# Moving two PSUM evictions to ScalarE and half of the rotary pass to GpSimd in a three-mixer decoder trunk

## The chip, the cores and the metric

The kernel runs on one core of a Trainium2 chip. The metric is device time in microseconds (us) of one execution, median over several executions. The engines in the text are TensorE (PE; its weight loads are listed apart as PEld), VectorE (DVE), ScalarE (ACT), GpSimd (POOL) and SyncE (SP), which issues all the transfers.

## The reference, cut to what matters

Two layers. Each projects the normalised stream h (1024 x 1024) to all queries, keys, values and gates, runs three groups of attention heads beside each other (A: differential attention, four heads with two softmaxes each; B: forgetting attention; C: stick-breaking attention), gates each output, applies one output projection and a layer norm. What the change touches is group A:

```python
r1 = x1 * cos - x2 * sin          # rotary, on the first 16 of 64 columns of q and k
r2 = x2 * cos + x1 * sin
...
w  = p1 - lam * p2                # two causal softmaxes of one head
oa = w @ v
oa = oa * rsqrt(mean(oa ** 2) + eps) * subln_g * (1 - lam_init)
ya = oa * silu(ag)
```

## The kernel before, in words

Everything is in blocks of 128 rows; SEQ is eight blocks. A projection (`proj_cols`, lines 150 to 161) makes one 128-column piece of q, k or a gate, transposed, in two halves of 512 positions; each half is 24 matmuls (weights and stream are split in a high and a low part) into one of two `acc` banks of PSUM, and is then evicted by `evac`. For group A `evac` of `proj_heads` (lines 233 to 247) applies the rotary embedding: DVE shuffles partitions out of the bank (`xy`, line 239), multiplies the bank by the cosine (`praw`, line 240), multiplies `xy` by the sine (line 241), and adds (line 242). Then `split_rows` (lines 177 to 185) splits `praw` in a rounded high part (ACT, line 181) and a rest (DVE, lines 183 and 185). There are four heads, q and k, two halves and two layers: 32 rotary passes. The `xy` tile has one buffer, which the gates share (tag `gate`), `praw` has two.

Attention of head m of group A (`attn_a`, lines 282 to 347) has five stages per block i: `soft` (two score products into `S` banks, DVE row maxima with the mask added, line 264; ACT exponentials, line 296; DVE combines the two softmaxes: reciprocal, `c`, and the mix into `e`, lines 299 to 301), `turn` (PE transposes `e` into `T` banks, line 275, evicted by ACT or DVE into `wT`), `mix` (i + 1 matmuls into a `T` bank `O_A`, evicted by DVE into `ou`, line 317), `close` (every fourth block: ACT squares, POOL power, DVE scaling of `ou`, line 334), `emit` (every fourth block: PE transposes four `ou` into a `T` bank `To_A`, which DVE evicts into `y` times a per-partition factor, line 344). All of `T`, `O_A` and `To_A` share two PSUM banks (tag `T`, line 60).

`advance` (line 633) emits the stages of five blocks at once, with the lags of line 43, between projections of the next head, which `FOLLOW` (line 556) lists:

```python
LAG = (0, 1, 2, 3, 5)
ORDER = {"A": (4, 3, 2, 0, 1), ...}
"C1": ("qA0", "kA0", "gC0"), "A0": ("qA1", "kA1", "vA2", "gC1"),
"A1": ("qA2", "kA2", "gA0"), "A2": ("qA3", "kA3", "vB0", "gA1"),
```

The framework then orders each engine's instructions by a plan of its own, made from the dependencies and its estimates of cost: each engine runs its queue strictly in that order, and the order is not the order of the code (instructions of `soft` stand between those of a rotary pass). POOL's other work is the low part of every weight tile (`wlo`, line 135, 128 x 512), the power of `close`, and parts of groups B and of the output stage.

Of the kernel before, what the change touches and what calls it, by code (L numbers as in the profile page):

```python
# [10 lines left out]
AF = mybir.ActivationFunctionType  # L11
ALU = mybir.AluOpType
# [3 lines left out]
P = 128  # L16
# [32 lines left out]
def tile_trunk(ctx, tc, x, ln_in_g, ln_in_b, w_in, b_forget, lambda_q1, lambda_k1, lambda_q2,  # L49
               lambda_k2, subln_g, w_out, ln_g, ln_b, c_ident, c_mask, c_tri, c_rope, out):  # L50
    nc = tc.nc
# [10 lines left out]
    def big(tag, name, shape=(P, S), dt=F32):  # L62
        return sb.tile(list(shape), dt, tag=tag, name=name, bufs=bufs[tag])

    def bank(tag, name, shape=(P, HALF)):
        return ps.tile(list(shape), F32, tag=tag, name=name, bufs=pbufs[tag])
# [3 lines left out]
    def mm(*args, **kw):  # L70
        recent[0] = nc.tensor.matmul(*args, **kw).ins  # L71
# [66 lines left out]
    def load_w(layer, col, n, key, tags=("whi", "wlo")):  # L138
        kn = 4 if n == P else 2
        res = []  # L140
        for k in range(0, NK, kn):
            raw = big("wraw", f"wr_{key}_{k}", (P, kn, n))
            src = w_in[layer, k * P:(k + kn) * P, col:col + n].rearrange("(k p) c -> p k c", p=P)
            nc.sync.dma_start(raw, src)
            hi, lo = split_w(raw, (P, kn, n), f"{key}_{k}", tags)
            res += [(hi[:, j, :], lo[:, j, :]) for j in range(kn)]
        return res


    def proj_cols(hts, w, evac, key):  # L150
        for half in range(2):
            hhi, hlo = hts[half]
            acc = bank("acc", f"acc_{key}_{half}")
            for k in range(NK):
                whi, wlo = w[k]
                mm(acc, lhsT=whi, rhs=hhi[:, k, :], start=k == 0, stop=False)
                mm(acc, lhsT=whi, rhs=hlo[:, k, :], start=False, stop=False)
                mm(acc, lhsT=wlo, rhs=hhi[:, k, :], start=False, stop=k == NK - 1)
                yield 0.65
            evac(half, acc)  # L160
            yield 0.0
# [15 lines left out]
    def split_rows(src, dst, cols, scale):  # L177
        for s in range(2):
            a, b = slice(64 * s, 64 * s + 64), slice(64 - 64 * s, 128 - 64 * s)
            hi = dst[s][a, cols]  # L180
            nc.scalar.activation(hi, src[a], AF.Copy, scale=scale)
            if scale == 1.0:
                nc.vector.tensor_tensor(dst[s][b, cols], src[a], f32(hi), ALU.subtract)
            else:
                nc.vector.scalar_tensor_tensor(dst[s][b, cols], src[a], scale, f32(hi), ALU.mult, ALU.subtract)
# [34 lines left out]
    def proj_heads(layer, hts, col, is_q, key, rope, done, tags):  # L220
        scale = QSCALE if is_q else 1.0
        res = [[None, None], [None, None]] if is_q else [None, None]
        def dest(half):
            if is_q:
                for s in range(2):
                    res[s][half] = big("Q1", f"Q1_{key}_{s}_{half}", (P, HALF), F32R)
                return [res[s][half] for s in range(2)], slice(0, HALF)
            if half == 0:
                for s in range(2):
                    res[s] = big("K", f"K_{key}_{s}", (P, S), F32R)  # L230
            return res, slice(half * HALF, (half + 1) * HALF)

        def evac(half, acc):
            src = acc
            if rope is not None:
                hs = slice(half * HALF, (half + 1) * HALF)
                src = big("praw", f"praw_{key}_{half}", (P, HALF))
                other = big("gate", f"xy_{key}_{half}", (P, HALF))
                nc.vector.stream_shuffle(other, acc, PARTNER)
                nc.vector.tensor_tensor(src, acc, rope[0][:, hs], ALU.mult)  # L240
                nc.vector.tensor_tensor(other, other, rope[1][:, hs], ALU.mult)
                nc.vector.tensor_tensor(src, src, other, ALU.add)
            d, cs = dest(half)
            split_rows(src, d, cs, scale)
            if half == 1:
                done(res)
        yield from proj_cols(hts, load_w(layer, col, P, key, tags=tags), evac, key)


    def scores(i, kst, q1, q2, key):  # L250
        half, rows = i // 4, slice((i % 4) * P, (i % 4 + 1) * P)
        res = []
        for a, b in row_pieces((i + 1) * P):
            sc = bank("S", f"S_{key}_{a}")
            mm(sc[:, :b - a], lhsT=q1[half][:, rows], rhs=kst[:, a:b], start=True, stop=False)
            mm(sc[:, :b - a], lhsT=q2[half][:, rows], rhs=kst[:, a:b], start=False, stop=True)
            res.append((a, b, sc[:, :b - a]))
        return res
# [23 lines left out]
    def attn_a(layer, head, kst, q1, q2, v, vcol, y, nlam, sg):  # L282
        key = f"A{layer}{head}"
        z1 = tiny.tile([P, NB], F32, tag="z1", name=f"z1_{key}", bufs=2)
        ws, wts, ous = {}, {}, {}

        def soft(i):
            n = (i + 1) * P
            es = []
            for s in range(2):  # L290
                k2 = f"{key}_{i}_{s}"
                sc = scores(i, kst[s], q1[s], q2[s], k2)
                e = big("e", f"e_{k2}")
                nm = neg_max(sc, mask[:, D + P - n:], e, k2)
                z = z1[:, i:i + 1] if s == 0 else tiny.tile([P, 1], F32, tag="z2", name=f"z2_{k2}")
                nc.scalar.activation(e[:, :n], e[:, :n], AF.Exp, bias=nm, scale=-1.0, accum_out=z)  # L296
                es.append(e)
            c = tiny.tile([P, 1], F32, tag="c", name=f"c_{key}_{i}")
            nc.vector.reciprocal(c, z)
            nc.vector.scalar_tensor_tensor(c, c, nlam, z1[:, i:i + 1], ALU.mult, ALU.mult)  # L300
            nc.vector.scalar_tensor_tensor(es[0][:, :n], es[1][:, :n], c, es[0][:, :n], ALU.mult, ALU.add)
            ws[i] = es[0]
            return 2 * SCORE_US[i]

        def turn(i):
            wts[i] = transposed(ws.pop(i), i, f"{key}_{i}")
            return 0.11 * (i + 1)

        def mix(i):
            wt = wts.pop(i)  # L310
            o = bank("T", f"O_{key}_{i}")
            for j in range(i + 1):
                mm(o[:, :P], lhsT=wt[:, j * P:(j + 1) * P], rhs=v[:, j, vcol:vcol + P],
                                 start=j == 0, stop=j == i)
            if i % 4 == 0:
                ous[i // 4] = big("ou", f"ou_{key}_{i}", (P, 4, P))
            nc.vector.tensor_copy(ous[i // 4][:, i % 4, :], o[:, :P])  # L317
            return 0.22 * (i + 1)

        def close(i):  # L320
            if i % 4 != 3:
                return 0.0
            ou, cs = ous[i // 4], slice(i - 3, i + 1)
            t = big("sq", f"sq_{key}_{i}", (P, HALF))
            ss = tiny.tile([P, 4], F32, tag="ss", name=f"ss_{key}_{i}", bufs=2)
            rs = tiny.tile([P, 4], F32, tag="rsa", name=f"rsa_{key}_{i}", bufs=2)
            for b in range(4):
                nc.scalar.activation(t[:, b * P:(b + 1) * P], ou[:, b, :], AF.Square, scale=P ** -0.5,  # L328
                                     accum_out=ss[:, b:b + 1])
            nc.vector.scalar_tensor_tensor(rs, z1[:, cs], EPS, z1[:, cs], ALU.mult, ALU.mult)  # L330
            nc.vector.tensor_tensor(rs, rs, ss, ALU.add)
            nc.gpsimd.tensor_tensor(rs, rs, mhalf, ALU.pow)
            for b in range(4):
                nc.vector.tensor_scalar(ou[:, b, :], ou[:, b, :], rs[:, b:b + 1], None, ALU.mult)
            return 0.0

        def emit(i):
            if i % 4 != 3:
                return 0.0
            ou = ous.pop(i // 4)  # L340
            t = bank("T", f"To_{key}_{i}")
            for b in range(4):
                nc.tensor.transpose(out=t[:, b * P:(b + 1) * P], in_=ou[:, b, :], identity=ident)
            nc.vector.tensor_scalar(y[:, (i - 3) * P:(i + 1) * P], t, sg, None, ALU.mult)
            return 0.44

        return [(i, soft, turn, mix, close, emit) for i in range(NB)]

    def attn_pair(layer, kind, pair, kst, q1, q2, v, y, negc=None):
# [223 lines left out]
    for layer in range(DEPTH):  # L573
# [51 lines left out]
        for n, tag in enumerate(("cos", "sin")):  # L625
            t = big(tag, f"{tag}_{layer}")
# [21 lines left out]
        for u, steps in FOLLOW.items():  # L648
# [5 lines left out]
            y = ys[u] if kind == "C" else big("y", f"y_{key}")  # L654
# [81 lines left out]
```

## Time and profile before

| what | us |
|---|---|
| median of 3 executions | 1378.75 (1377.78 to 1380.84) |
| the profiled execution, its own time | 1378.63 |
| its span (first to last instruction) | 1376.8 |
| busy: PE, DVE, ACT, POOL | 1329.1, 855.8, 575.7, 306.9 |
| mean granted TensorE clock | 0.998 of full |

The span is what the trace covers; 1.8 us of the execution's time lie around it. Busy times of the engines overlap. In this program PE is busy nearly throughout, so that a wait of PE adds to the time directly.

### The profile page before, as it was taken

Reading aid. Unit: us, or ns where it says so; the run is one execution under the profiler, and the core shown is the slowest. Engines: PE = TensorE matmul, PEld = TensorE weight load, DVE = VectorE, ACT = ScalarE, POOL = GpSimd, SP = SyncE. Lnnn points to the kernel's source line nnn. Section 1 sums busy time; section 2 is a strip of 40 time slices with the busy share of each in tenths; the row PEclk is TensorE's granted clock in tenths of the full one; section 3 lists DMA queues with packets and bytes.
Section 4 is the critical chain, followed back from the end, with each engine's and each line's share of the span. In section 5 each row is a group of like instructions: output and inputs, shape, how many; then the busy total and the mean of one; then the engine's idle time right before and its main releaser. Section 6 shows DMA issues by size and latency. Waiting matters only on the chain.

```text
span 1376.8 us, 21869 instructions
## 1 busy us (share of the span) xinstructions
PE 1329.1 (97%) x8250; PEld 1129.3 (82%) x8250; DVE 855.8 (62%) x1898; ACT 575.7 (42%) x1325; POOL 306.9 (22%) x309
## 2 busy tenths in 40 slices
PE   5999999999999999999999999999999999999997
PEld 4878878987898888777898897889887988877886
DVE  6644476569765775856542537675878567667554
ACT  2344454435343544641214444444444445456200
POOL 3410201121202222123422111112111222221332
PEclk9999999999999999999999999999999999999999
DMA  7550211032204131343435211112122132233342
GB/s 259 168 147 22 58 43 55 25 85 53 67 17 108 47 84 55 95 149 118 132 124 145 55 36 50 55 47 54 54 62 51 48 92 62 62 100 108 121 140 83
DMA packets 115569, 114.87 MB, mean 83 GB/s; under 512 B 8644, under 2 KB 93576, under 8 KB 115464
## 3 DMA queue, kind: packets, MB, share of 16 engines
q1 hardware_dynamic: 115464, 113.48, 27.9%
q8 instruction: 65, 1.06, 0.3%
q14 instruction: 40, 0.33, 0.1%
HBM read 74.62 MB, written 22.05 MB: 70 GB/s over the span
## 4 chain that ended last, share of the span: by engine, by line
PE 42%; DVE 5%; issue 4%; DMA 1%; ACT 1%; POOL 0%; SPq 0%; DVEq 0%; ACTq 0%; POOLq 0%
PE aco_o L71 12%; PE acc_qA L71 3%; PE acc_ggA L71 3%; PE S_A L71 2%; PE O_A L71 2%; PE acc_kA L71 2%; PE acc_ggB L71 2%; PE acr_vvA L71 2%; PE acc_kB L71 2%; PE acc_ggC L71 2%; PE O_B L71 1%; PE acc_qB L71 1%; PE S_B L71 1%; PE acr_vvB L71 1%; PE acc_kC L71 1%
## 5 line engine op out<-in xcount | busy, mean ns | idle before, releaser
L71 PE MATMUL aco_o<-wo,yhi_o 128*128 128x512 f32 (+1 forms) x462 | 142.0, 389 | 0.0
L296 ACT ACTIVATE e_A<-e_A,nm_A 128x256 f32<-128x256 f32 (+7 forms) x128 | 98.9, 773 | 32.4 <-DVE nm_A L264 31.6
L71 PEld LDWEIGHTS aco_o<-wo,yhi_o 128*128 128x128 f32 x462 | 85.5, 188 | 19.1
L372 DVE TENSOR_TENSOR_SCAN f_C<-f_C,mask 128x128 f32<-128x128 f32 (+7 forms) x64 | 85.5, 1376 | 24.7 <-ACT f_C L370 24.5
L71 PE MATMUL acr_vvA<-whi_vvA,hT 128*128 128x256 f32 x512 | 95.0, 283 | 0.0
L71 PE MATMUL aco_o<-wo,ylo_o 128*128 128x512 f32 (+1 forms) x231 | 89.7, 388 | 0.0
L71 PE MATMUL S_A<-K_kA,Q_qA 128*128 128x384 f32 (+3 forms) x384 | 86.1, 358 | 0.0
L71 PE MATMUL acc_qA<-hT,whi_qA 128*128 128x512 f32 x256 | 82.6, 401 | 0.0
L71 PE MATMUL acc_ggA<-hT,whi_ggA 128*128 128x512 f32 x256 | 82.2, 400 | 0.0
L71 PE MATMUL acc_kA<-hT,whi_kA 128*128 128x512 f32 x256 | 82.2, 401 | 0.0
L71 PEld LDWEIGHTS acr_vvA<-whi_vvA,hT 128*128 128x128 f32 x512 | 79.6, 188 | 0.2
L71 PEld LDWEIGHTS O_A<-v_vA,wT_A 128*128 128x128 f32 x576 | 73.2, 194 | 3.4
L71 PE MATMUL O_A<-v_vA,wT_A 128*128 128x128 f32 x576 | 75.7, 277 | 0.0
L328 ACT ACTIVATE sq_A<-ou_A 128x128 f32<-128x128 f32 x64 | 19.9, 311 | 126.0 <-DVE ou_A L317 126.0
L71 PE MATMUL acr_vvA<-wlo_vvA,hT 128*128 128x256 f32 x256 | 72.1, 282 | 0.0
L264 DVE CUSTOM_DVE_ANT_0 e_A<-S_A,mask 128x512 f32<-128x512 f32 (+3 forms) x128 | 68.5, 554 | 2.8 <-PE S_A L71 1.2
L509 POOL TENSOR_TENSOR ylo_o<-yr_o,yhi_o 128x256 fp32r<-128x256 f32 (+2 forms) x48 | 41.1, 883 | 118.0 <-ACT yhi_o L508 118.0
L71 PEld LDWEIGHTS S_A<-K_kA,Q_qA 128*128 128x128 f32 x384 | 63.1, 191 | 5.0 <-issue 0.7
L370 ACT ACTIVATE f_C<-S_C 128x384 f32<-128x384 f32 (+3 forms) x96 | 40.3, 494 | 57.5 <-PE S_C L71 57.3
L364 ACT ACTIVATE e_B<-e_B,nm_B 128x1024 f32<-128x1024 f32 (+7 forms) x64 | 49.5, 775 | 30.8 <-DVE nm_B L264 30.8
L360 POOL TENSOR_TENSOR negc<-negc,mask 128x128 f32<-128x128 f32 x64 | 34.2, 537 | 116.5 <-DVE nm_B L264 91.1
L526 DVE SCALAR_TENSOR_TENSOR r_o<-r_o,aco_o 128x512 f32<-128x512 f32 (+1 forms) x33 | 22.1, 671 | 58.0 <-PE aco_o L71 58.0
(213 smaller groups left out, 3433.8 us busy)
## 6 DMA issues: line engine op xcount, KB each, us to landing
Q_qA<-Q_qA SPq DMA_DIRECT2D x64, 128.0 KB, 2.4
wor<-in_w_out_dram SPq DMA_DIRECT2D x32, 256.0 KB, 2.6
r_o<-h_dram SPq DMA_DIRECT2D x16, 512.0 KB, 3.3
h_dram<-x SPq DMA_DIRECT2D x8, 512.0 KB, 4.3
wr_vvA<-in_w_in_dram SPq DMA_DIRECT2D x16, 256.0 KB, 2.7
Q_qC<-Q_qC SPq DMA_DIRECT2D x32, 128.0 KB, 2.4
wr_qA<-in_w_in_dram SPq DMA_DIRECT2D x16, 256.0 KB, 2.9
wr_kA<-in_w_in_dram SPq DMA_DIRECT2D x16, 256.0 KB, 2.9
```

Of the source, the lines that this page charges most:

```text
L71: recent[0] = nc.tensor.matmul(*args, **kw).ins
L264: nc.vector.tensor_tensor_reduce(e[:, a:b], sc, other[:, a:b], -1.0, lowest, ALU.add, ALU.min, nm)
L296: nc.scalar.activation(e[:, :n], e[:, :n], AF.Exp, bias=nm, scale=-1.0, accum_out=z)
L328: nc.scalar.activation(t[:, b * P:(b + 1) * P], ou[:, b, :], AF.Square, scale=P ** -0.5, accum_out=ss[:, b:b + 1])
L360: nc.gpsimd.tensor_tensor(diag, diag, mask[:, D:], ALU.add)
L364: nc.scalar.activation(w[:, :n], w[:, :n], AF.Exp, bias=nm, scale=-1.0, accum_out=z)
L370: nc.scalar.activation(w[:, a:b], p, AF.Sigmoid, scale=-1.0)
L372: nc.vector.tensor_tensor_scan(fr, fr, mask[:, :n], 0.0, ALU.mult, ALU.max)
L509: nc.gpsimd.tensor_tensor(ylo[:, e0:e0 + en, :], raw, f32(yhi[:, e0:e0 + en, :]), ALU.subtract)
L526: nc.vector.scalar_tensor_tensor(r[:, c0:c1], r[:, c0:c1], ALPHA, acc, ALU.mult, ALU.add)
```

## The change

`O_A` and `To_A` are evicted by ACT and not by DVE; the product with the sine and the sum of the rotary pass are made by POOL and not by DVE. The operands, the shapes and the rest of the program stay.

```diff
@@ proj_heads, evac
                 nc.vector.stream_shuffle(other, acc, PARTNER)
                 nc.vector.tensor_tensor(src, acc, rope[0][:, hs], ALU.mult)
-                nc.vector.tensor_tensor(other, other, rope[1][:, hs], ALU.mult)
-                nc.vector.tensor_tensor(src, src, other, ALU.add)
+                nc.gpsimd.tensor_tensor(other, other, rope[1][:, hs], ALU.mult)
+                nc.gpsimd.tensor_tensor(src, src, other, ALU.add)
@@ attn_a, mix
-            nc.vector.tensor_copy(ous[i // 4][:, i % 4, :], o[:, :P])
+            nc.scalar.copy(ous[i // 4][:, i % 4, :], o[:, :P])
@@ attn_a, emit
-            nc.vector.tensor_scalar(y[:, (i - 3) * P:(i + 1) * P], t, sg, None, ALU.mult)
+            nc.scalar.activation(y[:, (i - 3) * P:(i + 1) * P], t, AF.Copy, scale=sg)
```

## Rows read from the trace of the kernel before

**Rows 1.** The page, part 1: busy us, share of the span, instructions.

```profile
PE 1329.1 (97%) x8250; PEld 1129.3 (82%) x8250; DVE 855.8 (62%) x1898; ACT 575.7 (42%) x1325; POOL 306.9 (22%) x309
```

**Rows 2.** Stages by windows: length, then busy (instructions) of PE, PEld, DVE, ACT, POOL.

```profile
962.00:1001.00 39.00, 36.67 (x210) 31.59 (x209) 31.34 (x85) 17.80 (x50) 7.32 (x6) 1.00 0.22 62
1001.00:1052.00 51.00, 49.38 (x265) 41.61 (x265) 40.40 (x101) 22.75 (x55) 8.91 (x7) 1.00 0.21 56
```

**Rows 3.** Waits of PE and its weight loads: us in total, times, longest.

```profile
PE T_A L275 <- DVE e_A L301: 5.1, 4, 1.9
PE T_A L275 <- DVE ou_A L317: 3.7, 6, 1.0
PE T_A L275 <- DVE y_A L344: 3.0, 2, 1.5
...
PEld T_A L275 <- DVE ou_A L317: 5.5, 6, 1.4
...
PEld T_A L275 <- DVE y_A L344: 3.4, 2, 1.7
```

**Rows 4.** Timeline, 1003 to 1009 us: start, length, instruction, idle before it.

```profile
1003.62 1.28 PE L71 MATMUL O_A<-v_vA,wT_A 128*128 128x128 f32 x10
...
1006.09 1.39 DVE L183 TENSOR_TENSOR K_kA<-praw_kA,K_kA 64x512 fp32r<-64x512 f32 x2
...
1008.42 0.44 PE L275 MATMUL T_A<-ident,e_A 128*128 128x128 f32 x2 [0.99 <-DVE ou_A L317]
```

**Rows 5.** Timeline, 1057 to 1063 us.

```profile
1058.22 0.60 PE L343 MATMUL To_A<-ident,ou_A 128*128 128x128 f32 x4
...
1059.26 1.29 ACT L181 ACTIVATE K_kA<-praw_kA 64x512 fp32r<-64x512 f32 x2 [3.01 <-DVE praw_kA L242]
...
1061.35 0.75 DVE L344 TENSOR_SCALAR y_A<-To_A,sg 128x512 f32<-128x512 f32 x1
...
1062.16 0.66 PE L275 MATMUL T_A<-ident,e_A 128*128 128x128 f32 x4 [1.51 <-DVE y_A L344]
```

**Rows 6.** Groups of instructions that the change moves: busy us, mean ns, idle before.

```profile
L317 DVE COPY ou_A<-O_A 128x128 f32<-128x128 f32 x64 | 18.3, 286 | 59.5 <-PE O_A L71 59.2
...
L241 DVE TENSOR_TENSOR xy_kA<-xy_kA,sin 128x512 f32<-128x512 f32 x16 | 12.5, 780 | 0.0
...
L344 DVE TENSOR_SCALAR y_A<-To_A,sg 128x512 f32<-128x512 f32 x16 | 11.9, 743 | 2.1 <-PE To_A L343 2.1
...
L242 DVE TENSOR_TENSOR praw_kA<-praw_kA,xy_kA 128x512 f32<-128x512 f32 x16 | 10.9, 684 | 0.1
```

**Rows 7.** Groups by form: ACT copies out of PSUM of the same shapes.

```profile
L277 ACT COPY wT_A<-T_A 128x512 f32<-128x512 f32 x40 | 22.8, 570 | 3.7 <-PE T_A L275 3.6
...
L277 ACT COPY wT_A<-T_A 128x128 f32<-128x128 f32 x8 | 2.1, 265 | 3.4 <-PE T_A L275 3.4
```

**Rows 8.** Timeline, 970 to 985 us, inside one rotary pass.

```profile
982.26 1.27 POOL L135 TENSOR_TENSOR wlo_qA<-wr_qA,whi_qA 128x512 fp32r<-128x512 f32 x1 [4.44 <-ACT whi_qA L134]
982.37 1.18 DVE L300 SCALAR_TENSOR_TENSOR c_A<-c_A,nlam,z_A 128x1 f32<-128x1 f32 x1
...
983.47 0.68 DVE L241 TENSOR_TENSOR xy_qA<-xy_qA,sin 128x512 f32<-128x512 f32 x1
984.07 0.60 DVE L301 SCALAR_TENSOR_TENSOR e_A<-e_A,c_A,e_A 128x384 f32<-128x384 f32 x1
...
984.74 0.44 PE L275 MATMUL T_A<-ident,e_A 128*128 128x128 f32 x2 [1.95 <-DVE e_A L301]
```

**Rows 9.** Line 300 by itself: ns minimum/median/maximum, first and last start.

```profile
L300 DVE SCALAR_TENSOR_TENSOR c_A<-c_A,nlam,z_A x64: 206/219/1231, 213.8 to 1160.3; 128x1 f32<-128x1 f32 x64
```

**Rows 10.** Line 239, the first of each rotary pass: ns, first and last start.

```profile
L239 DVE STREAM_SHUFFLE xy_qA<-acc_qA x16: 729/738/749, 160.9 to 1040.3; 128x512 f32<-128x512 f32 x16
...
L239 DVE STREAM_SHUFFLE xy_kA<-acc_kA x16: 723/740/747, 179.8 to 1054.9; 128x512 f32<-128x512 f32 x16
```

**Rows 11.** Waits of the weight loads in group C.

```profile
PEld T_C L275 <- DVE f_C L372: 0.2, 1, 0.2
```

## The prediction, made before the changed kernel was run

> **What bounds the kernel.** I read the busy shares first: PE is busy for 97% of the span, no other engine for more than 62% [rows 1]. So the time is PE's work, which the change leaves alone, plus PE's waits, and only a wait that goes or comes counts. Next, the stages: while heads 1 and 2 of group A run beside the projections of heads 2 and 3, DVE is busy for 31.3 of 39 us and 40.4 of 51 us, against ACT's 17.8 and 22.8 and POOL's 7.3 and 8.9 [rows 2]. That is where DVE can be late for PE, and the waits say so: the transposes `T_A` wait for DVE's mix `e_A` (5.1 us, four times), for its eviction `ou_A` (3.7 us, six times) and for its eviction `y_A` (3.0 us, twice) [rows 3]. Both layers show the same pattern, so half of each belongs to a layer.
>
> The last two are waits for a PSUM bank, not for data, and the timeline shows why they arise. `O_A` is finished at 1004.9, yet its bank is still taken at 1008.4, since DVE's queue has the split `K_kA` (1.39 us, two of them) and more ahead of the copy; PE stands still for 0.99 us [rows 4]. `To_A` is finished at 1058.8, its eviction starts at 1061.35, and PE waits 1.51 us [rows 5]. The waits for `e_A` are different: they end with the chain row maximum, exponential, `c`, mix [rows 8].
>
> **The change, part by part.**
>
> *What leaves DVE.* 64 copies of 0.286 us, 16 evictions of 0.743 us, and 32 passes of a product and a sum; at 0.780 and 0.684 us (the k half's means, a little above the q half's) those are 46.8 us [rows 6, 10]. In all 18.3 + 11.9 + 46.8 = 77 us of DVE's 855.8. None of it is a saving by itself; it pays only where DVE is late for PE.
>
> *What ACT gets.* The same shapes out of PSUM took ACT 0.265 and 0.570 us [rows 7]: 64 x 0.265 + 16 x 0.570 = 26 us, ACT then being at 602 us, or 44%. What hides it is ACT's idleness: in the example it sat idle for 3.01 us before 1059.26, waiting for the rotary sum [rows 5], and `To_A` was ready at 1058.8. Put there, the eviction would be over at 1059.4, long before PE asks at 1060.65 (1062.16 less 1.51). The reader of `ou`, the square of `close`, is on ACT already and loses a wait for another engine. DVE's 59.2 us of idling ahead of line 317 [rows 6] move to ACT; what is queued behind that wait there are exponentials of scores that PE makes after `O_A` anyhow, and casts of weights.
>
> The gain is thus the eight bank waits. PE's own idle rows give 3.7 + 3.0 = 6.7 us; the weight loads of the same transposes give 5.5 + 3.4 = 8.9 us [rows 3]. A busy PE row runs on to a modelled end, so the first is too small, and the second counts the load's own lead; I take the middle, **7.8 us**, and keep 1 to 8.9 as the ends. The low end is an ACT queue in which the eviction stands behind the two splits, so that the bank comes free about as late as now. What is late next, after the bank? In neither example the data: the first four transposes of the same weights had gone ahead in rows 4, and in rows 5 only the bank is named.
>
> *What POOL gets.* 32 products and 32 sums of 128 x 512. POOL's product-like instruction of that shape, `wlo`, took 1.27 us [rows 8], so 2.54 us a pass and 81 us in all, POOL going to 388 us of 1376.8. A pass, from shuffle to sum, becomes at least 0.74 + 2.54 = 3.3 us where DVE's four instructions need 0.74 + 3 x 0.6 to 0.7, about 2.7. The split and the swap transfers of q start 0.6 us later; they hide behind the value or gate projection that stands before the next head's first scores. The accumulator bank is freed by shuffle and cosine product, both still DVE's: nothing changes there. POOL's queue now has the passes between its `wlo`s; those wait for ACT's casts with 4.44 us to spare in the example [rows 8].
>
> *The port.* Here is what can spoil it. `c_A`, 128 x 1, takes 0.219 us as a rule, and 1.231 us at worst [rows 9]; in rows 8 it takes 1.18 us, starts while POOL's `wlo` runs (982.26 to 983.53) and ends with it. So a DVE instruction with both inputs in SBUF stands still until POOL's is through. [...]
>
> What it costs: DVE's order inside a pass is shuffle, cosine product, `c`, sine product, mix, sum. The cosine product reads PSUM and isn't held. After the change `c` comes to the port 0.6 us after POOL's product began and waits 1.27 - 0.60 = 0.67 us; the sine product's 0.60 us (983.47 to 984.07, [rows 8]) that stood ahead of the mix is gone. If DVE gets the port between POOL's product and its sum, the mix starts 0.07 us later than now: nothing. I take that, since no `c` was held for longer than one POOL instruction (1.231 - 0.219 = 1.0 us, [rows 9]). So the 5.1 us for `e_A` stay. The ends: they all go (-5.1), or the mix is held for the sum as well (below).
>
> In group C, 8 passes run beside scans that have two SBUF inputs, too. A scan held once is 1.0 us later; but PE waited for a scan a single time, 0.2 us [rows 11]. Ends 0 and 8; I take **1 us** for new waits there and elsewhere, nearer to the row with the slack.
>
> *Sum*, against the profiled execution's own 1378.63, which is 0.12 below the median: 1378.63 - 7.8 + 1.0 = **1371.8 us**.
>
> **The rivals.**
>
> 1. *Slower: the port is not given back between POOL's two instructions.* The sum is queued behind the product and its other input is long there, so it may take the port at once; then the mix waits for the sum also, 0.07 + 1.27 = 1.34 us later. `c` and the mix stand inside 10 of the 32 passes where DVE is behind (five a layer, the first at 973.2, the last at 1054.9 in the second). There PE waits for the mix already or nearly: 10 x 1.34 = 13.4 us, and 1378.63 + 13.4 - 7.8 + 1.0 = 1385.2. It decides from 6 such passes on. For it: the waits for `e_A`, up to 1.9 us [rows 3], lie in these very passes. Against: rows 9. [...]
> 2. *No change: the evictions are late on ACT as well.* ACT's splits wait for the rotary sum, which now comes from POOL, behind a `wlo` at times. If the plan puts the eviction after them, the bank is free at about 1061, as now. Gain 1, cost 1: 1378.6. For it: DVE's plan had it just so [rows 5]. Against: ACT's 3 us idle there.
> 3. *More: DVE's backlog dissolves.* With 77 us less, the `e_A` waits go also: 1378.63 - 8.9 - 5.1 = 1364.6. Against: these waits come from passes in which the port, not DVE's load, decides.
>
> That the change doesn't do what it says (an extra table load on ACT, say) is hardly open: copies with a scale and without run on ACT in this stage already.
>
> **How the numbers follow.** A difference of 0.2%, 2.8 us, is about what a measurement of this kernel can tell from none. Chances: forecast 0.45, rival 3 0.13, rival 2 0.22, rival 1 0.20. The forecast's own range is 1369.7 (8.9 gained, nothing new) to 1376 (6.7 gained, 4 us new). The range for 8 in 10 goes from rival 3's 1364 to 1384, just short of rival 1's full price. Faster: 0.45 + 0.13 = 0.58; within 0.2%: 0.22; slower: 0.20.
>
> **What would show it right or wrong.** Right: no wait of `T_A` for `ou_A` or `y_A`, on DVE or on ACT, worth 1 us; waits for `e_A` near 5 us; `c_A`'s median above 0.219 us, with holds of 0.7 us; rotary instructions of 1.27 us on POOL. Rival 1 shows as waits of `T_A` for `e_A` well over 10 us and a mix that starts after POOL's sum; rival 2 as waits of `T_A` for ACT's `ou_A` and `y_A`; rival 3 as no wait for `e_A`. It would be wrong altogether if PE's waits moved to weights (`wlo` late on POOL) or to the score products' queries.

## The result, and the profile after

The changed kernel takes **1394.3 us** (median of four runs, 1391.4 to 1397.0) against 1379.8 us for the kernel before (four runs). The ratio is 1.011, 95% interval 1.0087 to 1.0134: it is slower, by 14.5 us, where 1371.8 had been forecast. The profiled execution took 1391.38 us, with a span of 1389.6.

The page's busy shares after, the same lines as in [rows 1] and in the same columns:

```profile
PE 1338.2 (96%) x8250; PEld 1135.5 (82%) x8250; DVE 799.2 (58%) x1754; ACT 602.1 (43%) x1405; POOL 392.1 (28%) x373
```

DVE lost 57 us of busy time, ACT gained 26, POOL 85: the work moved as meant (77 us had been counted off DVE; the mixing and the scans took some back, below). PE's count is the same, but its rows are 9 us longer in all, and it stands still for longer. Its waits after the change (us in all, times, longest), which answer to [rows 3]:

```profile
PE T_C L275 <- DVE y_C L390: 6.9, 6, 1.5
PE O_A L71 <- ACT wT_A L277: 3.8, 4, 1.6
...
PE acr_vvB L71 <- ACT whi_vvB L134: 2.5, 2, 1.3
PE T_A L275 <- DVE e_A L301: 2.3, 2, 1.1
...
PE acr_vvB L71 <- POOL wlo_vvB L135: 2.0, 2, 1.0
```

The waits of `T_A` for `ou_A` are gone, and that for `y_A` is down to 0.3 us, as forecast. New ones took their place, and they are elsewhere: `T_C` in group C waits for the bank that DVE's `y_C` has to free, the products `O_A` wait for ACT's copies `wT_A`, and the value projection of group B waits for weights. The stage of group C in the first layer shows it, by windows (length, then busy time and instructions of PE, PEld, DVE, ACT, POOL; the figure behind POOL's is the granted clock, as a share of full speed). In the kernel before:

```profile
155.00:205.00 50.00, 49.58 (x326) 39.39 (x325) 37.04 (x50) 24.02 (x53) 5.52 (x4) 1.00 0.13 35
```

and in the changed kernel:

```profile
155.00:205.00 50.00, 45.91 (x292) 35.93 (x292) 30.03 (x40) 21.15 (x47) 15.31 (x12) 1.00 0.12 32
```

In the same 50 us PE gets 34 instructions less done, and is idle for 4.1 us instead of 0.4. And yet no engine is fuller than before, except POOL, which is at 15.3 of 50. So it is not a lack of engine time. DVE and ACT are both less busy, and both late. The timeline of one pass in that window shows one of the waits (start, length, instruction, and in brackets the idle time before it with what ended it):

```profile
161.31 1.28 POOL L241 TENSOR_TENSOR xy_qA<-xy_qA,sin 128x512 f32<-128x512 f32 x1 [9.40 <-DVE xy_qA L239]
...
162.67 1.28 POOL L242 TENSOR_TENSOR praw_qA<-praw_qA,xy_qA 128x512 f32<-128x512 f32 x1
...
163.37 0.44 PE L71 MATMUL O_C<-wT_C,dv 128*64 128x128 f32 x4
...
163.98 1.28 ACT L181 ACTIVATE Q_qA<-praw_qA 64x512 fp32r<-64x512 f32 x2 [4.11 <-POOL praw_qA L242]
...
164.64 1.41 DVE L185 SCALAR_TENSOR_TENSOR Q_qA<-praw_qA,Q_qA 64x512 fp32r<-64x512 f32 x2 [2.85 <-ACT Q_qA L181]
...
166.08 0.29 DVE L390 TENSOR_TENSOR y_C<-y_C,O_C 128x128 f32<-128x128 f32 x1
...
166.42 0.44 PE L275 MATMUL T_C<-ident,f_C 128*128 128x128 f32 x2 [1.50 <-DVE y_C L390]
```

POOL's two instructions end at 163.95. ACT's half of the split is next in ACT's queue and has waited 4.11 us for them; DVE's difference is next in DVE's queue and has waited 2.85 us for ACT's half. Behind it stands `y_C`, whose `O_C` was made at 163.8, and behind that PE. Neither queue passes over the instruction that waits.

But the delay alone isn't the whole of this wait. The same pass in the kernel before:

```profile
164.19 2.02 DVE L185 SCALAR_TENSOR_TENSOR Q_qA<-praw_qA,Q_qA 64x512 fp32r<-64x512 f32 x2 [0.70 <-ACT Q_qA L181]
...
165.06 0.71 PE L71 MATMUL acc_qA<-hT,whi_qA 128*128 128x512 f32 x2
...
166.07 0.40 PE L275 MATMUL T_C<-ident,f_C 128*128 128x128 f32 x2
...
166.24 0.29 DVE L390 TENSOR_TENSOR y_C<-y_C,O_C 128x128 f32<-128x128 f32 x1
```

`y_C` came 5.37 us after the shuffle of the pass then and comes 5.59 us after it now, 0.2 us later. What differs is PE's order. Before, four matmuls of the projection stood ahead of these `T_C`, which started before `y_C` and so did not wait for it; now they come first and do. In the last pass of the window it is DVE's order that differs. Before, `y_C` stood ahead of the split:

```profile
190.23 1.31 PE L71 MATMUL O_C<-wT_C,dv 128*64 128x128 f32 x20
...
191.62 0.29 DVE L390 TENSOR_TENSOR y_C<-y_C,O_C 128x128 f32<-128x128 f32 x1 [0.29 <-PE O_C L71]
...
192.02 1.41 DVE L183 TENSOR_TENSOR K_kA<-praw_kA,K_kA 64x512 fp32r<-64x512 f32 x2
```

and in the changed kernel it stands behind it, 3.2 us after its `O_C` was made instead of 0.1:

```profile
193.35 1.31 PE L71 MATMUL O_C<-wT_C,dv 128*64 128x128 f32 x20
...
196.42 1.40 DVE L183 TENSOR_TENSOR K_kA<-praw_kA,K_kA 64x512 fp32r<-64x512 f32 x2 [3.45 <-ACT K_kA L181]
...
197.86 0.29 DVE L390 TENSOR_TENSOR y_C<-y_C,O_C 128x128 f32<-128x128 f32 x1
...
198.20 0.44 PE L275 MATMUL T_C<-ident,f_C 128*128 128x128 f32 x2 [1.27 <-DVE y_C L390]
```

Of the six waits of `T_C` for `y_C`, the four longest (1.50, 1.49, 1.27 and 1.28 us over the two layers) are at these two places; the two of 0.7 us come with both orders as they were, and there `y_C` is 0.6 us later in its pass. So the plan that the framework makes anew for each kernel has a part in the loss: it puts work behind a split that then waits. No run keeps the old order with POOL in the pass, so how much is the longer pass and how much the new order stays open.

Over the 32 passes, the waits of the split's two sides (engine and line, what is waited for, us in all, times, longest), first on ACT:

```profile
ACT Q_qA L181 <- POOL praw_qA L242: 77.0, 16, 7.5
ACT K_kA L181 <- POOL praw_kA L242: 54.8, 16, 4.8
```

and on DVE:

```profile
DVE Q_qA L185 <- ACT Q_qA L181: 34.7, 12, 3.7
DVE K_kA L183 <- ACT K_kA L181: 25.9, 14, 3.5
```

ACT's 131.8 us were 53.4 before (then a wait for DVE's sum), DVE's 60.6 were 13.2. The groups of the kernel before (busy us, mean ns, idle before):

```profile
L183 DVE TENSOR_TENSOR K_kA<-praw_kA,K_kA 64x512 fp32r<-64x512 f32 x32 | 25.5, 798 | 6.3 <-ACT K_kA L181 5.4
...
L185 DVE SCALAR_TENSOR_TENSOR Q_qA<-praw_qA,Q_qA 64x512 fp32r<-64x512 f32 x32 | 24.5, 766 | 8.5 <-ACT Q_qA L181 7.8
...
L181 ACT ACTIVATE K_kA<-praw_kA 64x512 fp32r<-64x512 f32 x32 | 20.1, 629 | 25.1 <-DVE praw_kA L242 24.6
L181 ACT ACTIVATE Q_qA<-praw_qA 64x512 fp32r<-64x512 f32 x32 | 20.1, 629 | 29.1 <-DVE praw_qA L242 28.8
```

DVE gave away 46 us of products and sums, and 47 us of waiting at the head of its queue came in their place.

In the experiments, **theory 1** is this: the splits, in their order behind a pass that has become longer, hold the queues of DVE and ACT. **Rival 1** is what the prediction calls the port, though no run shows one: POOL's instructions make DVE's longer. **Rival 2** is its second as well: the evictions are late on ACT. Each time stands against the kernel before as run on the same chip.

### The profile page after: what moved, and what is told of

The parts are those of the page before. It is cut to its first block, busy times and chain, and to the rows that moved or that the text cites. A ratio compares the mean times of both kernels' runs of the same rounds, so it can differ in the third digit from the quotient of the medians.

```text
span 1389.6 us, 21886 instructions
## 1 busy us (share of the span) xinstructions
PE 1338.2 (96%) x8250; PEld 1135.5 (82%) x8250; DVE 799.2 (58%) x1754; ACT 602.1 (43%) x1405; POOL 392.1 (28%) x373
## 3 DMA queue, kind: packets, MB, share of 16 engines
q1 hardware_dynamic: 115464, 113.48, 27.6%
## 5 line engine op out<-in xcount | busy, mean ns | idle before, releaser
L372 DVE TENSOR_TENSOR_SCAN f_C<-f_C,mask 128x128 f32<-128x128 f32 (+7 forms) x64 | 87.9, 1413 | 24.9 <-ACT f_C L370 24.8
L301 DVE SCALAR_TENSOR_TENSOR e_A<-e_A,c_A,e_A 128x128 f32<-128x128 f32 (+3 forms) x64 | 62.6, 978 | 2.0
L71 PE MATMUL acr_vvB<-whi_vvB,hT 128*128 128x260 f32 x256 | 52.3, 299 | 3.9 <-ACT whi_vvB L134 2.5
```

The costliest lines, as they stand in the source:

```text
L372: nc.vector.tensor_tensor_scan(fr, fr, mask[:, :n], 0.0, ALU.mult, ALU.max)
```

## The experiments

**One half each.** The evictions alone (line 317, line 344):

```diff
-            nc.vector.tensor_copy(ous[i // 4][:, i % 4, :], o[:, :P])
+            nc.scalar.copy(ous[i // 4][:, i % 4, :], o[:, :P])
...
-            nc.vector.tensor_scalar(y[:, (i - 3) * P:(i + 1) * P], t, sg, None, ALU.mult)
+            nc.scalar.activation(y[:, (i - 3) * P:(i + 1) * P], t, AF.Copy, scale=sg)
```

> Both evictions (O_A and the transposed outputs) by ScalarE, the rotary pass left whole on VectorE. Theory 1 (the loss comes from the rotary pass alone: the two splits behind it wait in order for GpSimd's product and sum, and what is queued behind them on VectorE and ScalarE is late for TensorE): faster than before by 4 to 10 us, about 1372 us, with no wait of TensorE on ou_A and none of T_C on y_C over 1 us. Rival 2 (the evictions are late at the head of ScalarE's queue, also without the rotary change): not faster than before, 1379 us or more, with TensorE's waits on ou_A and y_A still there, now named ACT.

Measured: 1371.06 us against 1378.86, ratio 0.9932 (0.9909 to 0.9955): 7.8 us faster. No wait on `ou_A` is left, none of `T_C` for `y_C` is among PE's waits, and of `y_A` 1.3 us remain, now on ACT (PE's waits):

```profile
PE T_A L275 <- DVE e_A L301: 3.6, 2, 1.8
...
PE T_A L275 <- ACT y_A L344: 1.3, 2, 0.6
```

The rotary part alone (lines 241 and 242, `nc.vector` to `nc.gpsimd`):

> Sine product and sum of the rotary pass by GpSimd, both evictions left on VectorE. Theory 1: slower than before by 12 to 22 us, about 1396 us, with the waits of VectorE's splits on ScalarE's half at about 60 us in all (13 before) and T_C waiting for y_C by several us. Rival 1 (the port is held, every VectorE instruction beside GpSimd's gets longer): slower too, but by VectorE's own durations: the scans, the differences and the mixing of e_A beside a pass are each longer by 0.5 us or more. Rival 2: within 3 us of before.

Measured: 1403.31 us against 1378.86, ratio 1.017 (1.0138 to 1.0202): 24.5 us slower, beyond the upper end of what theory 1 gave. DVE's splits wait 61.5 us (37.1 + 24.4), and `T_C` waits 6.9 us for `y_C`. The two halves add up to +16.7, and the whole change cost +14.5. So rival 2 is out, and all of the loss is in the rotary part. On rival 1 this run is mixed: the mixing of `e_A` takes 62.6 us instead of 54.3 (0.13 us more each), the scans 87.9 instead of 85.5; both are longer, neither by the 0.5 us that rival 1 asked for.

**The splits moved out of the way.** The changed kernel, with the splits of a pass (and the swap transfers) issued behind DVE's and ACT's last instruction of the score step that comes next:

```diff
+            def rest(): split_rows(src, d, cs, scale); return done(res) if half == 1 else None
+            if rope is None: rest()
+            else: late.append(rest)
-            split_rows(src, d, cs, scale)
-            if half == 1:
-                done(res)
...
+            with tc.issue_after(tail['dve']) if behind else ExitStack():
+                with tc.issue_after(tail['act']) if behind else ExitStack():
+                    late.pop(0)()
```

> The changed kernel, whole, with one thing moved: the two splits of a rotary pass (and the swap transfers of q that follow them) are issued behind VectorE's and ScalarE's last instruction of the score step that comes next, so that they no longer stand ahead of work that is ready. GpSimd does as much at much the same times. Theory 1: most of the loss comes back, 1371 to 1382 us, the splits' waits fall from 132 us (ScalarE) and 61 us (VectorE) to under half, and T_C waits for y_C by under 2 us. Rival 1 (the port): as slow as the changed kernel, 1390 to 1397 us, for the port is held as long. Rival 2 (evictions late on ScalarE): no gain either.

Measured: 1370.25 us against 1378.86, ratio 0.9929 (0.9903 to 0.9954), just under the range. All of the loss is back, with POOL doing as much as in the changed kernel. ACT's wait for POOL's sum in the q passes is 3.4 us in all, for 77.0, and DVE's splits wait 2.0 us, for 60.6. ACT's wait:

```profile
ACT Q_qA L181 <- POOL praw_qA L242: 3.4, 6, 1.1
```

That speaks for theory 1, but not yet against rival 1: the place may be a gain of its own.

**POOL's load without the wait.** The kernel before, with two more instructions on POOL behind each sum, into a tile that nobody reads:

```diff
+                nc.gpsimd.tensor_tensor(idle, src, rope[1][:, hs], ALU.mult); nc.gpsimd.tensor_tensor(idle, idle, src, ALU.add)
```

> The kernel before, whole, with two more 128x512 instructions of GpSimd (a product and a sum) behind each rotary pass, into a tile that nobody reads: GpSimd's load of the change without the wait on it. Theory 1: within 3 us of before, 1377 to 1382 us, with the splits' waits as before (13 us on VectorE). Rival 1 (the port): slower by 8 us or more, near the changed kernel.

Measured: 1430.0 us against 1378.86, ratio 1.0363 (1.033 to 1.0396), 51 us slower. Theory 1 was wrong here, and by far. The splits' waits are as before (7.8 and 6.4 us), but the splits themselves have become longer (busy us, mean ns, idle before):

```profile
L183 DVE TENSOR_TENSOR K_kA<-praw_kA,K_kA 64x512 fp32r<-64x512 f32 x32 | 45.4, 1420 | 7.1 <-ACT K_kA L181 6.4
L185 DVE SCALAR_TENSOR_TENSOR Q_qA<-praw_qA,Q_qA 64x512 fp32r<-64x512 f32 x32 | 42.7, 1334 | 8.6 <-ACT Q_qA L181 7.8
```

Before they took 798 and 766 ns. So POOL's instructions have a high price where they meet the splits: 38 us on 64 of them. But in the changed kernel these very splits take 740 and 686 ns, less than before, for they run after POOL's sum by construction. This run shows what rival 1 can cost, and not what it cost in the change.

**Late splits without POOL.** As the late split, with product and sum back on DVE:

> As the late split (both evictions by ScalarE, the splits of a pass issued behind the next score step), but sine product and sum stay on VectorE: GpSimd has no part in the pass. Theory 1 as it stands (a split that is ready costs nothing where it stood): about the time of the evictions alone, 1369 to 1373 us, so that the late split is worth something only where the product is late, and GpSimd's help is then worth nothing, -1 to +1 us against the late split with GpSimd. Its rival (the new place is itself a gain of 5 us or more, and the late split with GpSimd won by it while GpSimd still cost that much): 1362 to 1366 us.

Measured: 1364.83 us against 1378.44, ratio 0.991 (0.9887 to 0.9932). The median is in the rival's range: the new place seems to be itself a gain. It is 13.6 us under the kernel before, and the repetition below 11.8, where the evictions alone were 7.8 under it; but the intervals overlap. DVE had waited for ACT's halves before the change, too (13.2 us), and that goes as well. But 1365 and 1370 came from two chips, hence, on one chip, the late split with POOL

> The late split with GpSimd once more, on one chip with the next: what GpSimd's help itself is worth once neither queue waits. If nothing: the two within 2 us of one another. If GpSimd on the port costs even so: this one 3 to 8 us the slower, with the mixing of e_A and the scans longer here by 10 us and 3 us in all, as the two earlier profiles have them (62.9 against 52.3 us, 89.3 against 85.5 us).

and without it

> The late split with the pass whole on VectorE, on one chip with the one before. If the late split is itself a gain: 1362 to 1367 us, 12 us or more under before, and faster than either kernel of the change. If the earlier median was the chip: 1369 to 1372 us.

Measured: 1367.43 and 1366.81 us against 1378.57, ratios 0.9919 (0.9892 to 0.9947) and 0.9911 (0.9885 to 0.9937). They are 0.6 us apart, with intervals more than 7 us wide: once no queue waits for it, these runs can't tell POOL's help from none. Beside POOL's pass DVE's scans and mixing get longer, which takes back a share of what DVE is relieved of. DVE's groups with POOL in the pass (busy us, mean ns, idle before):

```profile
L372 DVE TENSOR_TENSOR_SCAN f_C<-f_C,mask 128x128 f32<-128x128 f32 (+7 forms) x64 | 89.3, 1435 | 31.5 <-ACT f_C L370 31.5
...
L301 DVE SCALAR_TENSOR_TENSOR e_A<-e_A,c_A,e_A 128x128 f32<-128x128 f32 (+3 forms) x64 | 62.9, 983 | 2.1
```

and without it:

```profile
L372 DVE TENSOR_TENSOR_SCAN f_C<-f_C,mask 128x128 f32<-128x128 f32 (+7 forms) x64 | 85.5, 1376 | 28.4 <-ACT f_C L370 28.4
...
L301 DVE SCALAR_TENSOR_TENSOR e_A<-e_A,c_A,e_A 128x128 f32<-128x128 f32 (+3 forms) x64 | 52.3, 818 | 1.9
```

These are 14.4 us more of scans and mixing against 44 us of products and sums that are gone; the splits take the same in both (932 and 878 ns with POOL, 933 and 884 without). PE's waits are 1 us or less for each of `T_A` and `T_C` in both. Both beat the kernel before and the changed one.

**Part of the move.** Both evictions on ACT, of the pass the sine product alone on POOL (line 241):

> Both evictions by ScalarE, and of the rotary pass the sine product alone by GpSimd; the sum stays on VectorE. Theory 1 (what counts is how long VectorE is held by the pass, busy or waiting): VectorE now waits for one GpSimd instruction (1.28 us) beside its own cosine product (0.74 us), so 0.6 to 0.8 us of wait in place of 0.6 to 0.78 us of work: 0 to 4 us over the evictions alone, 1371 to 1375 us. Rival 1 (the port, by GpSimd's busy time): half of the loss of the whole move, 1381 to 1385 us.

Measured: 1385.17 us against 1378.44, ratio 1.0051 (1.0032 to 1.0069), 14.5 us above the evictions alone, each against its own kernel before. Theory 1 had 0 to 4, and rival 1's number came out. The rows of the pass give less than half of it, 6.7 us by the account below: DVE's sum now waits for POOL, which is worse than the product it gave away, and the k half's sum is itself held, at 1229 ns instead of 684 [rows 6]. DVE's waits in this kernel:

```profile
DVE praw_qA L242 <- POOL xy_qA L241: 15.2, 14, 1.8
...
DVE praw_kA L242 <- POOL xy_kA L241: 8.3, 8, 1.5
```

and the group of the k half's sums:

```profile
L242 DVE TENSOR_TENSOR praw_kA<-praw_kA,xy_kA 128x512 f32<-128x512 f32 x16 | 19.7, 1229 | 8.5 <-POOL xy_kA L241 8.3
```

So 23.5 us of waiting and 8.8 us of holding replaced 23.8 us of products. I had counted a wait of 0.6 to 0.8 us and got 1.1 (15.2/14). The 8.8 us are rival 1's mechanism. PE's list has 4.3 us of waits of `T_C` for `y_C` here, which the evictions alone don't have, and 6.3 for 3.0 us for the bank that DVE's cosine product frees for the value projection of group B. Theory 1 as it stood did not foresee the size of this run.

**The wait without POOL.** Both evictions on ACT, the pass whole on DVE, and an in-place copy by ACT ahead of the splits:

```diff
+                nc.vector.tensor_tensor(src, src, other, ALU.add); nc.scalar.copy(src, src)
```

> Both evictions by ScalarE, rotary pass whole on VectorE, and one in-place copy of the rotated half by ScalarE ahead of its splits: VectorE's splits come about 0.6 us later in each of the 32 passes, with GpSimd idle. Theory 1 (the in-order wait alone): slower than the evictions alone by 8 us or more, 1379 to 1388 us, with TensorE waiting for y_C by some us in the stage of the scans. Rival 1 (the wait alone is cheap, the loss needs GpSimd on the port): 1369 to 1374 us.

Measured: 1380.4 us against 1378.44, ratio 1.0015 (1.0003 to 1.0027), so 9.8 us over the evictions alone, each against its own kernel before. In time theory 1 holds: 0.6 us of lateness in 32 passes costs 10 us with POOL out of the pass; but ACT has 19.8 us of copies more to do here, and no run takes the two apart. In place it missed: the copies changed the planned order in group C (in the first pass `y_C` now stands ahead of the split), and PE's waits came with `e_A` (5.7 us) and not with `y_C`.

**One queue freed at a time.** The changed kernel with DVE's two differences alone issued late; ACT's halves stay:

```diff
-            def rest(): split_rows(src, d, cs, scale); return done(res) if half == 1 else None
+            split_rows(src, d, cs, scale, "both" if rope is None else "hi")
+            def rest(): split_rows(src, d, cs, scale, "lo") if rope is not None else None; return done(res) if half == 1 else None
```

> The changed kernel with VectorE's two differences of a pass alone issued behind the next score step (the swap transfers with them); ScalarE's two halves stay where they are, right behind the pass, and ScalarE still waits for GpSimd there. If the hold of VectorE's queue is what costs: most of the loss comes back, 1369 to 1378 us, with ScalarE's wait for the sum still over 100 us. If the hold of ScalarE's queue is (its copies of wT and its casts of weights come late): 1385 us or more. In between: both, in that measure.

Measured: 1408.57 us against 1378.57, ratio 1.0211 (1.018 to 1.0242): nothing comes back, it is 15.5 us worse than the change. DVE's splits no longer wait (1.7 us in all), but ACT's stand at the head of its queue for 140 us (131.8 in the changed kernel), and now DVE waits for what is behind them there. DVE's waits:

```profile
DVE c_A L299 <- ACT e_A L296: 61.3, 52, 4.7
...
DVE f_C L372 <- ACT f_C L370: 48.2, 29, 4.2
```

and one of PE's:

```profile
PE T_C L275 <- ACT wT_C L277: 10.5, 6, 3.5
```

These were 49.3, 24.8 and 1.5 us in the changed kernel. By what was written ahead of the run, this is the result that puts the loss on ACT's queue. Then the other way round: ACT has no part in the pass, DVE makes the rounded halves (`on_dve` is set for the rotary passes):

```diff
-            nc.scalar.activation(hi, src[a], AF.Copy, scale=scale)
+            nc.vector.tensor_scalar(hi, src[a], scale, None, ALU.mult) if on_dve else nc.scalar.activation(hi, src[a], AF.Copy, scale=scale)
```

> The changed kernel with the two rounded halves of each rotary pass made by VectorE, where they stand, in place of ScalarE: ScalarE has no part in the pass and its queue never waits for GpSimd; VectorE is held as long as before or longer (it waits for GpSimd's sum, about 0.7 us less per pass, and then does two halves more, up to 0.7 us each). If ScalarE's hold is the larger part of the loss: faster than the changed kernel's 1394 us in spite of up to 44 us more work on VectorE, 1376 to 1390 us, the vvB projection no longer waiting for whi_vvB or wlo_vvB. If VectorE's hold is: 1396 us or more (some 0.6 us more in each of 32 passes), with T_C waiting longer for y_C than the changed kernel's 6.9 us.

Measured: 1422.57 us against 1378.02, ratio 1.0312 (1.0283 to 1.034), 30.1 us worse than the change. By what was written ahead of it, this one puts the loss on DVE's queue: both count, and relieving one alone did not pay, here at 42 us more of work on DVE. `T_C` waits 12.8 us for `y_C` (6.9 in the changed kernel), and the pass's rows on DVE show a wait for POOL and then more work:

```profile
L181 DVE TENSOR_SCALAR K_kA<-praw_kA 64x512 fp32r<-64x512 f32 x32 | 22.2, 692 | 21.7 <-POOL praw_kA L242 21.2
...
L181 DVE TENSOR_SCALAR Q_qA<-praw_qA 64x512 fp32r<-64x512 f32 x32 | 19.9, 622 | 30.2 <-POOL praw_qA L242 25.4 <-DMA wr_kA<-in_w_in_dram 4.3
```

**An account of held time.** For each kernel I added up, over DVE's rows of the 32 passes (lines 181, 183, 185 and 239 to 242, of qA and kA, the loading of the shuffle's mask left out), the busy time and the idle time before them: how long a pass holds DVE's queue, at work or waiting. To that come the scans (372) and the mixing (301), which get longer beside POOL's instructions. The time is the median less that of the kernel before on the same chip.

| kernel | busy | waiting | held | scans, mixing | sum | time |
|---|---|---|---|---|---|---|
| before | 140.9 | 15.2 | 156.1 | 139.8 | 295.9 | 0 |
| evictions alone | 138.0 | 15.4 | 153.4 | 139.0 | 292.4 | -7.8 |
| rotary alone | 93.1 | 65.4 | 158.5 | 150.5 | 309.0 | +24.5 |
| changed kernel | 90.8 | 67.2 | 158.0 | 150.5 | 308.5 | +14.5 |
| sine product alone, evictions | 120.0 | 37.6 | 157.6 | 141.5 | 299.1 | +6.7 |
| wait by ACT, evictions | 137.1 | 25.9 | 163.0 | 139.0 | 302.0 | +2.0 |
| halves by DVE | 131.2 | 53.9 | 185.1 | 151.0 | 336.1 | +44.6 |
| POOL's load alone | 177.9 | 16.1 | 194.0 | 151.4 | 345.4 | +51.1 |
| late splits, POOL | 103.2 | 2.5 | 105.7 | 152.2 | 257.9 | -11.1 |
| late splits, no POOL | 147.4 | 2.9 | 150.3 | 137.8 | 288.1 | -11.8 |
| only DVE's splits late | 97.0 | 2.0 | 99.0 | 152.6 | 251.6 | +30.0 |

The change took 50 us of work from DVE's passes and left the held time where it was, 158.0 for 156.1. In three comparisons sum and time go together: POOL's load alone +49.5 and +51.1; halves by DVE over the changed kernel +27.6 and +30.1; the wait by ACT over the evictions alone +9.6 and +9.8. None of the three touches DVE alone: POOL is loaded in the first, ACT loses its halves in the second and gets copies in the third. They part in the last row, where ACT's queue is the one that is late, and with the late splits and POOL, where DVE's sum is 30 us lower than without POOL and the time the same: there DVE is no longer what PE waits for.

For the change itself, over the evictions alone, the sum gives +16.1 and the time is +22.3. The 6 us that lack are not settled (for the sine product alone it is 7.8, for the rotary part alone 11.4). Two things lie there. One is ACT's queue: waits of PE for `wT_A`, `whi_vvB` and, behind that cast, `wlo_vvB` come to 8.3 us in the changed kernel and aren't on the list of the evictions alone. At one of them ACT waits 4.59 us for POOL's sum, makes its halves from 383.63 and the cast of `whi_vvB` only at 384.94; in the kernel before that cast stood ahead of the halves (372.88 and 376.66), so here, too, the order is new. The other is PE's clock: at 386.7 us, after a wait of 1.25 us for those weights and 0.7 us into the next of 0.98, the granted clock fell from 1.00 to 0.50 of full speed (the means of 380 to 386.7 and of 386.7 to 390 us). The window 290 to 395 us of the changed kernel has a mean of 0.97, where the kernel before has 1.00:

```profile
290.00:395.00 105.00, 99.24 (x540) 84.91 (x540) 70.22 (x173) 50.57 (x133) 41.42 (x31) 0.97 0.21 57
```

So the time is not PE's work plus its waits at one clock. Whether the waits brought the drop no run shows; if they did, a wait of PE costs more than its own length. Between the profiled executions of the kernel before and of the changed kernel the span grows by 12.8 us, and 9.1 of them are PE's rows, which take 1338.2 us for 1329.1 at a mean clock of 0.993 for 0.998; the evictions alone had 0.997. The account leaves this out, also where it agrees: with POOL's load alone the mean clock was 0.985. It is a measure that goes with the time, and no proof that the held time is the whole cause.

## Why the prediction was wrong

**The evictions: right, in kind and size.** 7.8 us were forecast and 7.8 measured, with the waits on `ou_A` gone. That the two agree to the tenth is luck: the interval reaches from 6 to 13 us, 1.3 us of the waits for `y_A` stayed, and 1.5 of those for `e_A` went, which were to stay. The price on ACT was 28 us, not 26: `y_A` took 685 ns, 115 more than the plain copy that I took for it [rows 7]. It differs from that copy by its scale, one value per partition; no run takes the 115 ns apart. The price stayed hidden. Table loads on ACT are four in both kernels. ACT's groups in the changed kernel:

```profile
L317 ACT COPY ou_A<-O_A 128x128 f32<-128x128 f32 x64 | 17.0, 265 | 72.8 <-PE O_A L71 72.5
L344 ACT ACTIVATE y_A<-To_A,sg 128x512 f32<-128x512 f32 x16 | 11.0, 685 | 1.7 <-PE To_A L343 1.7
```

**POOL's price: right.** 1.28 to 1.34 us for each instruction, 1.27 forecast; two of its four groups:

```profile
L242 POOL TENSOR_TENSOR praw_kA<-praw_kA,xy_kA 128x512 f32<-128x512 f32 x16 | 21.4, 1340 | 0.9
L241 POOL TENSOR_TENSOR xy_qA<-xy_qA,sin 128x512 f32<-128x512 f32 x16 | 20.6, 1289 | 53.8 <-DVE xy_qA L239 53.8
```

**The step that failed** is this sentence: "The split and the swap transfers of q start 0.6 us later; they hide behind the value or gate projection that stands before the next head's first scores." It asks who needs the split's result, and that is indeed not soon. It doesn't ask what is queued behind the split, nor whether the plan keeps its order. The 0.6 us were about right: a pass in group C, from shuffle to the end of its splits, takes 5.95 us after and 5.48 before, on the mean of eight over both layers. But DVE now stands still for 3.0 us of them ahead of its differences (0.4 before), and ACT, in the pass shown above, for 4.1 us ahead of its halves; what had been done in between, or comes behind, is late. In all DVE's splits wait 60.6 us for 13.2 and ACT's 131.8 for 53.4, and the rotary part alone costs 24.5 us where the forecast had 1. [Rows 5] had shown the pattern: there ACT's split waits 3.01 us for the sum, and DVE's next work stands behind. I used that row for the eviction only.

**Group C: 1 us forecast, taken for scans that are held.** Measured by windows, PE idles 3.7 us more in the 50 us from 155, and from 829 to 880 us, in the second layer, 3.9 more (46.67 us busy for 50.53). I looked for a late scan [rows 11], and the scans are 0.04 us longer each on the mean; one scan that is held is later by what I had counted (at 151.13 us of the kernel before, 128x128 beside a `wlo`: 1.42 us, where the shortest scan takes 0.39). The wait came by way of `y_C`, which stands behind the split, in one of the passes only since the change; it was 0.7 us in the weight loads before, too small to be looked at.

**The port: the forecast of no gain and no loss for `e_A` was wrong by little, for other reasons.** The port is the prediction's name; what the traces show is which instructions stood still. In the kernel before, all six `c_A` that began while a `wlo` ran took 1.17 to 1.23 us, against a median of 0.219, and ended 0.02 us after it; the four splits of q that did took 1.30 to 1.34 us, against 0.69. The cosine product, which reads PSUM, took 0.67 to 0.69 us in all 32 passes, 0.67 also at 328.16 us, with a `wlo` from 328.10 to 329.40. Where DVE's had begun first it was POOL's that took longer: at 181.78 us the sum took 0.69 us, and the `wlo` beside it, from 181.94, 1.66 instead of 1.27. The waits fell from 5.1 to 2.3 us. `c_A` wasn't held more: its longest went from 1231 to 880 ns, at the same median. What is held is the mixing, 978 ns on the mean for 849. The largest price was seen where POOL's instructions met others with two inputs in SBUF: 0.57 to 0.62 us on each split beside POOL's load alone, and 0.55 us on each of the k half's sums with the sine product alone.

**The rivals.** Rival 1 had the sign, and with 1385.2 the nearest time, but the loss came another way: the mix was held by POOL's sum, as it says, eight times in the changed kernel (at 248.58 us it took 1.73 us, against 0.75), and yet the waits for `e_A` didn't pass 10 us, they came to 2.3. Rival 2 is refuted by the evictions alone, rival 3 by the time and by the 2.3 us of waits for `e_A` that stayed. Of the last sentence of the prediction a part came true: 4.5 us of PE's waits moved to weights, `whi_vvB` and `wlo_vvB`, since the cast now stands behind a split on ACT. A rival "the split, in a new order, holds the queues" was missing, and the range ended at 1384 for that.

## What to carry to other kernels

When a step in the middle of a chain goes to a slower engine, don't count what the first engine is relieved of; count how long the chain's last instruction there stands at the head of its queue, busy or waiting, and look at what is queued behind it, on every engine that the chain comes back to, in the order that the changed kernel has: a plan that is made anew may put other work there. Here 50 us less work left DVE held as long as before and ACT longer. With the move, only the version whose chain's end was issued behind work that was ready lost nothing (1367.4 us), and the one without the move was as fast: both evictions on ACT, pass on DVE, splits late, 1366.8 us.

## What was not expected of the hardware

Where POOL's two-input instructions met DVE's, both got longer on the mean. Beside POOL's two extra instructions DVE's splits took 1.33 and 1.42 us instead of 0.77 and 0.80, and POOL's extra sum, against 1.28 to 1.34 us for the sum of the pass in the changed kernel, took 1.6 to 1.7. The row maxima, which read PSUM and one SBUF tile, were untouched: 554 ns in both kernels. Which of the two stood still, these means can't tell. POOL's groups with its load alone:

```profile
L243 POOL TENSOR_TENSOR idle_qA<-idle_qA,praw_qA 128x512 f32<-128x512 f32 x16 | 27.1, 1693 | 0.9
L243 POOL TENSOR_TENSOR idle_kA<-idle_kA,praw_kA 128x512 f32<-128x512 f32 x16 | 25.7, 1605 | 1.1
```

With the queues out of the way, moving 44 us of work from DVE to POOL made 0.6 us of difference (1367.43 and 1366.81 us). What DVE loses beside POOL's instructions is 14.4 us in these two runs, in the scans and the mixing.
